# The backward half of the scan's decay weight, formed on VectorE instead of GpSimd

## The chip, the cores and the metric

The kernel runs on one core of a Trainium2 chip. The metric is the device time of one execution in microseconds (us), taken as the median of several runs. A core has five engines that run side by side, each through its own instruction list in order: TensorE (PE in the profile; PEld is its weight load), VectorE (DVE), ScalarE (ACT), GpSimd (POOL) and SyncE (SP), which here only issues DMA transfers. An engine that waits holds up everything behind the waiting instruction in its own list.

## The reference

One inference step of a four-layer backbone over 384 tokens (128 context tokens and 256 latent ones, model width 1024). Layers 0 and 3 mix tokens with a two-way state-space scan (SSD), layer 1 with a short convolution, layer 2 with differential attention; a gated convolutional FFN follows each. For the scan the reference forms, for each chunk of 128 tokens and each of 32 heads, a forward pass

```
decay  = exp(where(mask, acs[q] - acs[s], -inf))      # acs: running sum of dt * a
cb     = einsum('bcqgn,bcsgn->bcqsg', c, b)           # per group of four heads
y_diag = einsum('bcqsgr,bcsgrp->bcqgrp', cb[..., None] * decay * dt[:, :, None], x)
y_off  = einsum('bcqgn,bcgrpn->bcqgrp', c, h_in) * exp(acs)[..., None]
```

and the same again backward over the flipped sequence with its own `dt`, and adds the two. The kernel merges both directions: for one chunk and four heads it needs a weight `w = (cb_lower * dt_fwd + cb_upper * dt_bwd) * e`, 128 by 512, with `e` the exponential of the decay.

## The kernel before

All matrix weights are streamed from memory in blocks of 128x1024 floats. Each is split into a high and a low part (`wh` on ACT at L155, `wl` on DVE at L156), and every product of the projections is three matmuls (L340, 24 of them for an output block of 128x384). Four rotating buffers hold raw blocks.

An SSD layer runs eight groups of four heads. While `scan` works on group g, the projections of group g+1 (four blocks that go through the three-tap convolution, L396 on ACT, L398 and L400 on DVE) and the gate of group g (two blocks) run on PE between the scan's small products. The blocks of all of these rotate through three PSUM banks (`mm`), and a bank is free for the next 24 matmuls when the convolution's last DVE instruction (L400) has read it.

`decay(t)`, called for the three chunks of a group, forms the weight: the backward product of the masked `cb` and the backward `dt` (L683), four exponents (L686 on DVE, L687 on ACT), four multiply-adds of the forward half (L690), and the product with `e` (L691). For t = 1 and 2 it also scales the carried-in states' factors (`ab`, L695 on ACT and L697 on DVE). `out` multiplies the weights with the tokens (L726, `yp`). `e` and `w` share one tag of four buffers.

Besides this, the adaLN modulation of the next layers is computed as filler: `unit` (L187, `modps`, four 512-column matmuls, eight records in the trace) reads a 1 MB block of `w_mod`. In the SSD stage all of these blocks pass through one buffer (`wm`, `WM = 1`), so a block can be loaded only when PE has read the one before it. The filler is dealt out evenly by `pace`, a call per group, but the order on every engine is not the order of the code: the program is built with `TileContext(nc, schedule_with_timeline_sim=True)` (L1017), and a scheduler in the build orders all engines' instructions by its own estimate of times. It therefore moves instructions of other engines too when one instruction changes its engine.

DMA transfers are issued by SP in that scheduled order: weight blocks, `wm`, the rows of `acs` (`ab`), carried-in states (`h`), and the writing of new states (`out_new_state`).

Of the kernel before, what the change touches and what calls it, by code (L numbers as in the profile page):

```python
# [14 lines left out]
ALU = mybir.AluOpType  # L15
# [4 lines left out]
P = 128  # L20
# [24 lines left out]
class Net:  # L45
# [570 lines left out]
    def ssd_core(self, l, j, keep, cw, dn, y, ssq):  # L616
        d, V, S, GP, PE = self.d, self.V, self.S, self.GP, self.PE
        h4 = lambda a: a.rearrange("p (h e) -> p h e", h=4)

        def convs(g, pr, out, tag="mm"):  # L620

            ch = self.cm_weights(2)
            for b in range(2):
                ps = self.cm_block(ch, 2, b, tag=tag)
                w = cw[:, g, 2 * pr + b]
                t = self.conv(ps, w)
                S.activation(t, t, AF.Silu, bias=w[:, 3:4])
                out.append(t)
                yield
# [20 lines left out]
        def scan(g, blocks):  # L650
# [22 lines left out]
            cb = pl.tile([P, 2, NT, P], F32, tag="cb", name="cb")  # L673
# [5 lines left out]
            def decay(t):  # L679

                per = lambda a, dr: a[:, t, dr * 32 + 4 * g:dr * 32 + 4 * g + 4, None].to_broadcast([P, 4, P])
                e, w = tt("e"), tt("w")
                GP.tensor_tensor(h4(w), cb[:, 1, t, None, :].to_broadcast([P, 4, P]), per(dt, 1), op=ALU.mult)  # L683
                for h in range(4):
                    hs, sl = 4 * g + h, slice(h * P, (h + 1) * P)
                    V.scalar_tensor_tensor(e[:, sl], abs_[t][:, 0, sl], dac[:, t, hs:hs + 1], abs_[t][:, 1, sl], op0=ALU.subtract, op1=ALU.min)  # L686
                    S.activation(e[:, sl], e[:, sl], AF.Exp, bias=nac[:, t, hs:hs + 1])  # L687
                for h in range(4):
                    hs, sl = 4 * g + h, slice(h * P, (h + 1) * P)
                    V.scalar_tensor_tensor(w[:, sl], cb[:, 0, t, :], dt[:, t, hs:hs + 1], w[:, sl], op0=ALU.mult, op1=ALU.add)  # L690
                V.tensor_tensor(w, w, e, op=ALU.mult)  # L691
                mv = [(xt[:, t, :], w)]
                if t:
                    ce = abs_[t]
                    S.activation(ce, ce, AF.Exp)  # L695
                    c3 = ce.rearrange("p r (h q) -> p (r h) q", h=4)
                    V.tensor_tensor(c3, c3, Cc[:, None, t * P:(t + 1) * P].to_broadcast([P, 8, P]), op=ALU.mult)  # L697
                    mv += [(hst[t, dr], ce[:, dr]) for dr in range(2)]
                return mv
# [31 lines left out]
            states(((1, 0), (2, 1)))  # L731
            hst.update({(1, 0): hin[0], (2, 0): new[0], (2, 1): hin[1], (1, 1): new[1]})
            mv0 = decay(0)
            yield
            states(((0, 0), (0, 1)))
            mv1 = decay(1)
            yp = [self.psum("yp") for _ in range(2)]
            out(0, mv0)
            mv2 = decay(2)
            yield  # L740
            out(1, mv1)
# [7 lines left out]
        with self.tc.tile_pool(name=f"steps{l}", bufs=1, reuse_waits="tile") as sp:  # L749
            dt, dac, nac, gd, wdt, dec = self.steps(j, keep, sp, lambda: list(convs(0, 0, cur)) + list(convs(0, 1, cur, "yp")))  # L750
# [273 lines left out]
```

## Time and profile before

| | us |
|---|---|
| median of three runs | 2422.38 (2415.94 to 2424.57) |
| the profiled execution | 2417.66 |
| its span in the profile | 2415.9 |
| PE busy | 2295.4 (95%) |
| DVE busy | 1621.2 (67%) |
| ACT busy | 1253.4 (52%) |
| POOL busy | 334.2 (14%) |

The profile is one execution, 1.8 us longer than its span. The two SSD stages lie at about 46 to 392 us and 1745 to 2083 us; the rest of the span is FFN, short convolution, attention and output projections, in which the changed line does not occur. A row of a timeline gives start, duration, engine, line, operation and, in brackets, how long the engine stood idle before it and what released it. Consecutive matmuls overlap, so a PE row's duration is longer than its distance to the next one.

### The profile page before, as it was taken

To read this page: it belongs to the slowest core of one execution; us is meant where nothing else is said; L and a number is where in the kernel's file an instruction comes from. 1 tells how busy PE (TensorE), PEld (TensorE's weight loads), DVE (VectorE), ACT (ScalarE), POOL (GpSimd) and SP (SyncE) were. 2 spreads that over 40 slices of the span, in tenths; PEclk is the share of its full clock that TensorE was granted. 3 is DMA by queue.
4 is the path that set the end of the run, shared out by engine and by line. 5 is a ranking of instruction groups with operands and counts; after the bars stand their busy time and mean duration, and the time that the engine had idled before them with its cause. 6 is when DMAs were issued, how large, how long until landed. Compare 5 with 4: busy or idle time off the path is not lost.

```text
span 2415.9 us, 35621 instructions
## 1 busy us (share of the span) xinstructions
PE 2295.4 (95%) x13132; PEld 2002.2 (83%) x13132; DVE 1621.2 (67%) x2930; ACT 1253.4 (52%) x2173; POOL 334.2 (14%) x498
## 2 busy tenths in 40 slices
PE   6989999899999999999999979999998999989998
PEld 3878887699987969998688649998687888779987
DVE  3787876577655457776655547776578888677765
ACT  3666765444444344444544444444556776554444
POOL 1122330100001010000123320000113323010000
PEclk7999999999999999999999999999999999989999
DMA  7556655533537564335435463335455654423442
GB/s 286 181 162 207 202 192 177 201 132 122 166 111 288 204 245 138 125 122 166 155 106 176 155 244 107 123 127 162 147 159 171 200 159 153 139 97 123 131 146 81
DMA packets 113374, 391.79 MB, mean 162 GB/s; under 512 B 13104, under 2 KB 25520, under 8 KB 100912
## 3 DMA queue, kind: packets, MB, share of 16 engines
q1 hardware_dynamic: 113200, 389.52, 49.2%
q8 instruction: 103, 1.69, 0.3%
q14 instruction: 71, 0.58, 0.1%
HBM read 382.39 MB, written 7.08 MB: 161 GB/s over the span
## 4 chain that ended last, share of the span: by engine, by line
PE 78%; DVE 9%; DMA 6%; ACT 3%; issue 2%; POOL 2%; SPq 0%; POOLq 0%; ACTq 0%; DVEq 0%
PE mm L340 44%; PE mm L380 20%; PE mm L811 4%; DMA wm<-in_w_mod 3%; PE modps L187 2%; PE yp L380 2%; DVE e L686 2%; DVE wl L156 1%; PE yp L726 1%; DVE w L690 1%; PE yp L852 1%; ACT jk L263 1%; DVE cv L398 1%; DMA wx<-in_w_mod 1%; PE yp L340 1%
## 5 line engine op out<-in xcount | busy, mean ns | idle before, releaser
L340 PE MATMUL mm<-hh,wh 128*128 128x384 f32 (+1 forms) x2352 | 796.4, 340 | 14.9 <-DVE cv L400 9.8
L340 PE MATMUL mm<-hl,wh 128*128 128x384 f32 (+1 forms) x2352 | 793.8, 338 | 0.0
L340 PE MATMUL mm<-hh,wl 128*128 128x384 f32 (+1 forms) x2352 | 792.0, 338 | 0.0
L156 DVE TENSOR_TENSOR wl<-wr,wh 128x1024 fp32r<-128x1024 f32 (+2 forms) x466 | 564.4, 1213 | 259.7 <-ACT wh L155 257.6
L155 ACT ACTIVATE wh<-wr 128x1024 fp32r<-128x1024 f32 (+2 forms) x466 | 483.3, 1039 | 313.1 <-PE mm L340 243.9
L340 PEld LDWEIGHTS mm<-hh,wh 128*128 128x128 f32 (+1 forms) x2352 | 443.3, 189 | 38.9 <-DVE cv L400 14.6
L340 PEld LDWEIGHTS mm<-hh,wl 128*128 128x128 f32 (+1 forms) x2352 | 442.3, 188 | 5.3 <-issue 3.4
L340 PEld LDWEIGHTS mm<-hl,wh 128*128 128x128 f32 (+1 forms) x2352 | 442.6, 188 | 4.5 <-issue 2.2
L396 ACT ACTIVATE cv<-mm,fcw 128x384 f32<-128x384 f32 x176 | 100.1, 571 | 233.4 <-PE mm L340 228.2
L380 PE MATMUL mm<-wh,gh 128*128 128x512 f32 x528 | 208.7, 395 | 0.0
L380 PE MATMUL mm<-wl,gh 128*128 128x512 f32 x528 | 208.6, 395 | 0.0
L380 PE MATMUL mm<-wh,gl 128*128 128x512 f32 x528 | 207.9, 395 | 0.0
L271 POOL TENSOR_SCALAR m<-s 128x1 f32<-128x1 f32 x42 | 17.2, 409 | 1145.5 <-ACT jk L263 1144.7
L398 DVE SCALAR_TENSOR_TENSOR cv<-mm,fcw,cv 128x127 f32<-128x127 f32 x352 | 144.1, 410 | 42.6 <-ACT cv L396 42.6
L405 ACT ACTIVATE gh<-fg 128x384 fp32r<-128x384 f32 x176 | 92.2, 524 | 152.6 <-PE mm L380 151.7
L406 DVE TENSOR_TENSOR gl<-fg,gh 128x384 fp32r<-128x384 f32 x176 | 97.6, 557 | 96.7 <-ACT gh L405 96.1
L400 DVE SCALAR_TENSOR_TENSOR cv<-mm,fcw,cv 128x127 f32<-128x127 f32 x352 | 145.8, 415 | 10.8
L380 PEld LDWEIGHTS mm<-wh,gh 128*128 128x128 f32 x528 | 99.0, 187 | 25.0 <-issue 0.8
L380 PEld LDWEIGHTS mm<-wh,gl 128*128 128x128 f32 x528 | 99.0, 187 | 24.2
L380 PEld LDWEIGHTS mm<-wl,gh 128*128 128x128 f32 x528 | 99.0, 187 | 23.9
L187 PE MATMUL modps<-wm,sil 128*32 128x512 f32 x496 | 78.3, 655 | 18.5 <-DMA wm<-in_w_mod 17.6
L683 POOL TENSOR_TENSOR w<-cb,dt 128x512 f32<-128x512 f32 x48 | 71.6, 1504 | 92.5 <-DVE w L691 91.6
(224 smaller groups left out, 3180.9 us busy)
## 6 DMA issues: line engine op xcount, KB each, us to landing
wr<-in_ffn_up SPq DMA_DIRECT2D x176, 512.0 KB
wm<-in_w_mod SPq DMA_DIRECT2D x62, 1024.0 KB
wr<-in_ssd_in SPq DMA_DIRECT2D x96, 512.0 KB
wr<-in_ffn_down SPq DMA_DIRECT2D x88, 512.0 KB
wx<-in_w_mod SPq DMA_DIRECT2D x34, 1024.0 KB
ab<-acs SPq DMA_DIRECT2D x48, 512.0 KB
wr<-in_ssd_out SPq DMA_DIRECT2D x32, 512.0 KB
wr<-in_sc_in SPq DMA_DIRECT2D x32, 384.0 KB
```

The costliest lines, as they stand in the source:

```text
L155: self.S.activation(hi[:, :m], raw[:, :m], AF.Copy)
L156: self.V.tensor_tensor(lo[:, :m], raw[:, :m], hi[:, :m].bitcast(F32), op=ALU.subtract)
L187: self.PE.matmul(acc[32 * j:32 * j + 32, :], self.sil[:, kb, :], raws[:, j // 2, (j % 2) * 512:(j % 2 + 1) * 512], start=kb == 0, stop=kb ...
L340: self.PE.matmul(acc[:m], w, h, start=n == 0, stop=n == len(ops) - 1)
L380: self.PE.matmul(acc[t], g[:, o:o + n], w, start=k == 0 and i == 0, stop=k == nk - 1 and i == 2)
L396: self.S.activation(t, src, AF.Copy, scale=cw[:, 1:2])
L398: self.V.scalar_tensor_tensor(t[:, o + 1:o + n], src[:, o:o + n - 1], cw[:, 0:1], t[:, o + 1:o + n], op0=ALU.mult, op1=ALU.add)
L400: self.V.scalar_tensor_tensor(t[:, o:o + n - 1], src[:, o + 1:o + n], cw[:, 2:3], t[:, o:o + n - 1], op0=ALU.mult, op1=ALU.add)
L405: self.S.activation(hi, src, AF.Copy)
L406: self.V.tensor_sub(lo, src, hi.bitcast(F32))
L683: GP.tensor_tensor(h4(w), cb[:, 1, t, None, :].to_broadcast([P, 4, P]), per(dt, 1), op=ALU.mult)
L811: PE.matmul(acc[t][:, :256], h[k][:, o:o + m], w[:, ws], start=k == 0 and i == 0, stop=k == KB - 1 and i == 2)
```

## The change

In `decay` the first product moves from GpSimd to VectorE; operands, result and buffer are the same. It occurs 48 times: three chunks, eight groups, two layers. GpSimd keeps the state products (L707, L717) and the sum of squares (L648).

```
-                GP.tensor_tensor(h4(w), cb[:, 1, t, None, :].to_broadcast([P, 4, P]), per(dt, 1), op=ALU.mult)
+                V.tensor_tensor(h4(w), cb[:, 1, t, None, :].to_broadcast([P, 4, P]), per(dt, 1), op=ALU.mult)
```

The scheduler then orders all engines anew. Three places show how.

The first is VectorE in layer 3, fifth group, the part of its list that ends with the release (the last L400 here) of the bank that PE's next 24 matmuls need. Before:

```order
L398 SCALAR_TENSOR_TENSOR cv<-mm,cw,cv 128x127
L690 SCALAR_TENSOR_TENSOR w<-cb,dt,w 128x128 x4
L400 SCALAR_TENSOR_TENSOR cv<-mm,cw,cv 128x127
L398 SCALAR_TENSOR_TENSOR cv<-mm,cw,cv 128x255
L686 SCALAR_TENSOR_TENSOR e<-ab,dac 128x128 x4
L156 TENSOR_TENSOR wl<-wr,wh 128x1024
L400 SCALAR_TENSOR_TENSOR cv<-mm,cw,cv 128x127
L398 SCALAR_TENSOR_TENSOR cv<-mm,cw,cv 128x255
L400 SCALAR_TENSOR_TENSOR cv<-mm,cw,cv 128x255
```

Now:

```order
L398 SCALAR_TENSOR_TENSOR cv<-mm,cw,cv 128x127
L400 SCALAR_TENSOR_TENSOR cv<-mm,cw,cv 128x127
L398 SCALAR_TENSOR_TENSOR cv<-mm,cw,cv 128x255
L683 TENSOR_TENSOR w<-cb,dt 128x512
L156 TENSOR_TENSOR wl<-wr,wh 128x1024
L686 SCALAR_TENSOR_TENSOR e<-ab,dac 128x128 x4
L400 SCALAR_TENSOR_TENSOR cv<-mm,cw,cv 128x127
L398 SCALAR_TENSOR_TENSOR cv<-mm,cw,cv 128x255
L400 SCALAR_TENSOR_TENSOR cv<-mm,cw,cv 128x255
L156 TENSOR_TENSOR wl<-wr,wh 128x1024
L398 SCALAR_TENSOR_TENSOR cv<-mm,cw,cv 128x127
L690 SCALAR_TENSOR_TENSOR w<-cb,dt,w 128x128 x4
```

The third chunk's product (L683) stands in this piece now, and the third chunk's four multiply-adds (L690) have gone behind the release. The products of the first two chunks stand earlier in the same group, each ahead of its exponents (L686).

The second place is TensorE in layer 3, second group; `wm_17795` and `wm_18171` are two successive blocks of the one `wm` buffer, `mm_17299` is the next projection block. Before:

```order
L187 MATMUL modps_17040<-wm_17795,sil_83 32x512 x4
L726 MATMUL yp_17219<-w_17202,xt_17059 64x128 x2
L726 MATMUL yp_17220<-w_17202,xt_17059 64x128 x2
L726 MATMUL yp_17219<-ab_17051,h0_17055 64x128 x2
L726 MATMUL yp_17220<-ab_17051,h0_17055 64x128 x2
L726 MATMUL yp_17219<-ab_17051,s_17137 64x128 x2
L726 MATMUL yp_17220<-ab_17051,s_17137 64x128 x2
L340 MATMUL mm_17299<-hh0_16119,wh_16948 128x384
L340 MATMUL mm_17299<-hl0_16121,wh_16948 128x384
```

Now:

```order
L187 MATMUL modps_17040<-wm_17795,sil_83 32x512 x4
L726 MATMUL yp_17219<-w_17202,xt_17059 64x128 x2
L726 MATMUL yp_17220<-w_17202,xt_17059 64x128 x2
L726 MATMUL yp_17219<-ab_17051,h0_17055 64x128 x2
L726 MATMUL yp_17220<-ab_17051,h0_17055 64x128 x2
L726 MATMUL yp_17219<-ab_17051,s_17137 64x128 x2
L726 MATMUL yp_17220<-ab_17051,s_17137 64x128 x2
L187 MATMUL modps_17040<-wm_18171,sil_83 32x512 x4
L726 MATMUL yp_17219<-w_17226,xt_17059 64x128 x2
L726 MATMUL yp_17220<-w_17226,xt_17059 64x128 x2
L726 MATMUL yp_17219<-ab_17053,s_17134 64x128 x2
```

Before, the projection follows the state products at once and the unit of `wm_18171` comes in the next group; now that unit, and the third chunk's products behind it, stand ahead of the projection.

The third place is TensorE in layer 3, fourth group, between the third and the fourth projection block. Before:

```order
L726 MATMUL yp_17971<-w_17954,xt_17811 64x128 x2
L726 MATMUL yp_17972<-w_17954,xt_17811 64x128 x2
L340 MATMUL mm_18051<-hh1_16120,wl_17838 128x384
L726 MATMUL yp_17971<-ab_17803,h0_17807 64x128 x2
L726 MATMUL yp_17972<-ab_17803,h0_17807 64x128 x2
L726 MATMUL yp_17971<-ab_17803,s_17889 64x128 x2
L726 MATMUL yp_17972<-ab_17803,s_17889 64x128 x2
L668 MATMUL tp_18189<-ident_120,cv_17872 128x128 x3
L187 MATMUL modps_17040<-wm_18547,sil_83 32x512 x4
L340 MATMUL mm_18109<-hh0_16119,wh_17843 128x384
```

Now:

```order
L668 MATMUL tp_18189<-ident_120,cv_17872 128x128 x3
L187 MATMUL modps_17040<-wm_19299,sil_83 32x512 x4
L726 MATMUL yp_17971<-w_17893,xt_17811 64x128 x2
L726 MATMUL yp_17972<-w_17893,xt_17811 64x128 x2
L726 MATMUL yp_17971<-w_17954,xt_17811 64x128 x2
L726 MATMUL yp_17972<-w_17954,xt_17811 64x128 x2
L726 MATMUL yp_17971<-ab_17803,h0_17807 64x128 x2
L726 MATMUL yp_17972<-ab_17803,h0_17807 64x128 x2
L726 MATMUL yp_17971<-ab_17803,s_17889 64x128 x2
L726 MATMUL yp_17972<-ab_17803,s_17889 64x128 x2
L187 MATMUL modps_17040<-wm_19523,sil_83 32x512 x4
L340 MATMUL mm_18109<-hh0_16119,wh_17843 128x384
```

Before there is one unit in this group; now there are two, with eight rows of `yp` products between them. The same shape (two units with only these products between) arises once in layer 0, in its fourth group. In five more groups a second unit now stands 24 projection matmuls behind the first. In layer 0's second group the third chunk's products now stand ahead of the projection block `mm_1263`, which they followed before.

## Rows read from the trace of the kernel before

**Rows 1.** Four regular groups: stretch, us, busy PE, PEld, DVE, ACT, POOL, clock, DMA.

```profile
1864.00:2005.10 141.10, 137.90 (x925) 124.46 (x924) 117.81 (x240) 99.12 (x166) 44.54 (x45) 1.00 0.59 179
```

**Rows 2.** Chain that ended last, layer 3's fourth group: start us, us, what.

```profile
1897.54 1.02 DVE cb L675 x2
...
1916.29 4.43 PE mm L340 x24
```

**Rows 3.** Waits of PE in layer 3's SSD stage: us in total, times, longest us.

```profile
PE mm L340 <- DVE cv L400: 4.0, 5, 0.8
```

**Rows 4.** Waits of PE in layer 0's SSD stage.

```profile
PE mm L340 <- DVE cv L400: 4.5, 4, 1.4
```

**Rows 5.** Groups by line and shape: busy us, mean ns, idle before them.

```profile
L686 DVE SCALAR_TENSOR_TENSOR e<-ab,dac 128x128 f32<-128x128 f32 x192 | 81.5, 483 | 0.0
L683 POOL TENSOR_TENSOR w<-cb,dt 128x512 f32<-128x512 f32 x48 | 71.6, 1504 | 92.5 <-DVE w L691 91.6 <-DVE cb L675 0.9
...
L691 DVE TENSOR_TENSOR w<-w,e 128x512 f32<-128x512 f32 x48 | 38.8, 814 | 9.2 <-ACT e L687 9.2
```

**Rows 6.** Timeline of VectorE, layer 3's fourth group.

```profile
1899.12 1.75 DVE L686 SCALAR_TENSOR_TENSOR e<-ab,dac 128x128 f32<-128x128 f32 x2
...
1901.46 1.65 DVE L686 SCALAR_TENSOR_TENSOR e<-ab,dac 128x128 f32<-128x128 f32 x6
...
1906.66 0.68 DVE L691 TENSOR_TENSOR w<-w,e 128x512 f32<-128x512 f32 x1
1907.26 1.21 DVE L156 TENSOR_TENSOR wl<-wr,wh 128x1024 fp32r<-128x1024 f32 x1
...
1908.66 1.26 DVE L691 TENSOR_TENSOR w<-w,e 128x512 f32<-128x512 f32 x1
...
1911.24 1.13 DVE L690 SCALAR_TENSOR_TENSOR w<-cb,dt,w 128x128 f32<-128x128 f32 x4
```

**Rows 7.** Timeline of GpSimd, the same group.

```profile
1898.64 2.09 POOL L683 TENSOR_TENSOR w<-cb,dt 128x512 f32<-128x512 f32 x2
```

**Rows 8.** Chain that ended last, layer 3's second group: a reload of `wm` and what follows.

```profile
1827.90 8.28 DMA wm<-in_w_mod
...
1836.22 1.94 PE modps L187 x8
1838.16 2.76 PE yp L726 x24
```

**Rows 9.** Timeline of PE, layer 0: two units 6.3 us of PE work apart.

```profile
282.18 1.06 PE L187 MATMUL modps<-wm,sil 128*32 128x512 f32 x8
...
290.94 1.06 PE L187 MATMUL modps<-wm,sil 128*32 128x512 f32 x8 [0.84 <-DMA wm<-in_w_mod]
```

**Rows 10.** Chain that ended last, whole span: other reloads, and layer 0's second group.

```profile
73.72 7.05 DMA wm<-in_w_mod
...
141.77 4.44 PE mm L340 x24
146.21 1.46 PE yp L726 x24
...
217.83 9.44 DMA wm<-in_w_mod
```

**Rows 11.** Busy time by stretch around the reload of rows 8.

```profile
1829.00:1834.00 5.00, 0.20 (x2) 0.20 (x4) 5.00 (x17) 2.07 (x5) 0.18 (x1) 0.74 0.73 245
...
1838.00:1841.00 3.00, 3.00 (x29) 2.58 (x25) 2.96 (x11) 2.73 (x5) 0.00 (x0) 0.50 0.27 83
```

**Rows 12.** Timeline of PE, layer 3's fourth group, from the state products on.

```profile
1911.97 0.66 PE L726 MATMUL yp<-w,xt 128*64 128x128 f32 x8
...
1914.43 1.06 PE L187 MATMUL modps<-wm,sil 128*32 128x512 f32 x8
1916.29 0.44 PE L340 MATMUL mm<-hh,wh 128*128 128x384 f32 x1 [0.80 <-DVE cv L400]
```

**Rows 13.** Timeline of VectorE, layer 0's second group, the third chunk's weight.

```profile
142.39 0.69 DVE L691 TENSOR_TENSOR w<-w,e 128x512 f32<-128x512 f32 x1 [1.90 <-ACT e L687]
```

## The prediction

> **What bounds the kernel now.** I read the busy time by stretch first, then the chain of waits, then who PE waits for, and last the timelines of the two engines that the product moves between. In four regular groups of layer 3's scan, 141.1 us, PE is busy for 137.9 us and VectorE for 117.8 us [rows 1]: PE is nearly full and VectorE is at 83%. The chain still runs through both. In each group it leaves PE with the `cb` masks (1897.54) and comes back at 1916.29, when the next 24 projection matmuls start [rows 2]. Over those 18.7 us VectorE works without a pause, and PE, busy with other blocks, arrives early by only 0.80 us [rows 12]. So the reader is to see two engines that finish almost together. All that PE waits for the convolution's bank (L400) is 4.0 us in layer 3's stage and 4.5 us in layer 0's [rows 3, 4]. A faster VectorE can give back 8.5 us and no more; anything that holds PE is paid almost whole.
>
> **The product itself.** 48 products leave GpSimd, 71.6 us of its busy time [rows 5], and join VectorE. VectorE has no row with such operands. The nearest is L691, same size and type, two SBUF inputs: 0.68 us long and 0.60 us from its start to the next start (1906.66 to 1907.26) [rows 6]. From above I bound it by 1.05 us, half of the two GpSimd products that ran in 2.09 us [rows 7]. From below there is no reason for less than L691 costs. I take L691's 0.60, three in a group: +1.8 us.
>
> **What VectorE gets back.** While GpSimd ran its two products (1898.64 to 1900.73), two L686 took 1.75 us; the next six took 1.65 us, 0.275 each [rows 6, 7]. Without GpSimd's products the two should take 0.55 us, so 1.2 us come back. The second L691 took 1.26 us against 0.68 for the first: 0.6 us more. That is 1.8 us in a group, as much as the product costs. The total says the same: L686 at 0.275 would need 52.8 us and not 81.5, L691 at 0.68 would need 32.6 and not 38.8; 34.9 us come back against 28.8 (48 at 0.60) to 50.4 (48 at 1.05). VectorE's load stays about equal.
>
> The Trainium skill ("SBUF — State Buffer", section "Who interferes with whom") says that a VectorE instruction with two SBUF inputs contends with a GpSimd instruction that reads SBUF, and that the one that comes second is blocked for the other's whole length. The trace agrees on the contention (0.87 us against 0.275 for an L686). By whole blocking the 48 products would give back up to 48 times 1.05, about 50 us of VectorE, an estimate; the rows show 34.9, and PE's 8.5 us caps both.
>
> The order changes too. In the stretch that ends with the bank's release, the third product comes in and the third chunk's four multiply-adds go behind the release; they took 1.13 us, 1.05 from start to start. The stretch becomes 18.7 + 1.8 - 1.8 - 1.05 = 17.7 us. That is below PE's own arrival, so most of the 8.5 us of waiting goes. I count -6 us for it, and -2 us because the state products now stand in fewer pieces between projections; bounds 0 and -10.5.
>
> **What the new order costs.** The filler units read one buffer. A unit cannot start until the block before it has been read and the next one has landed. Reloads in the chain took 7.05, 8.28 and 9.44 us [rows 8, 10]. The tightest regular pair had its second unit start 7.7 us after the end of the first (283.24 to 290.94), after a wait of 0.84 us with 6.3 us of PE work in between [rows 9]. I take 7.7 us, bounds 7.05 and 9.44. Five effects follow, all on PE, whose list is in order:
>
> - Layer 3, second group. The unit of `wm_17795` ended at 1838.16 and the state products at 1840.92 [rows 8]; projections followed at once. Now the next unit stands there. It cannot start before 1838.16 + 7.7 = 1845.9: PE idles 4.9 us (4.3 to 6.7). The clock is still low: it was 0.74 over the idle stretch 1829 to 1834 and 0.50, the 1.2 GHz level, over 1838 to 1841 [rows 11], and an idle PE will keep it there. At that level a unit took 1.94 us [rows 8] and not the 1.06 of rows 9, and 24 state products took 2.76 us and not the 1.46 of rows 10. So the unit and the 24 state products behind the new wait cost about 0.9 + 1.3 = 2.2 us more. Sum 7.1 us.
> - Layer 3, fourth group, the pair of `wm_19299` and `wm_19523`. Between them stand 24 state products, some 2.0 us by the distance 1911.97 to 1914.43 less a transpose [rows 12]. PE idles 7.7 - 2.0 = 5.7 us, of which 0.8 was idle before: 4.9 us. Five idle microseconds brought the clock down in rows 11, so 2.2 us more: 7.1 us. The second unit's own time is no addition, since another group loses it.
> - Layer 0, fourth group, the same shape: 7.1 us.
> - Five pairs with 24 projection matmuls and the state products between them, about 6.4 us of work. At the 0.84 us of rows 9 each this is 4.2 us, of which 0.84 existed already. Net 3.4 us (-0.8 to 14).
> - Layer 0, second group. The projection that ran from 141.77 [rows 10] now follows the third chunk's products, whose weight was ready at 142.39 + 0.69 = 143.08 [rows 13]: 1.3 us.
>
> **Sum.** 7.1 + 7.1 + 7.1 + 3.4 + 1.3 = 26.0 us, less 8 us, is +18.0 us. On the profiled execution (2417.66 us; its span is 2415.9) this gives 2435.7 us. The median of the three runs lies 4.7 us above that execution, so from there it would be 2440.4. I forecast 2437 us, between the two. With the lower bounds (7.05 us, no clock loss, nothing at the five pairs and in layer 0's second group) the three large waits are 4.3 + 4.25 + 4.25 = 12.8 us, less 10.5: 2420. With the upper (9.44 us: 8.9 + 8.8 + 8.8 + 14 + 1.3, nothing back) it is +42: 2460.
>
> **Rivals.**
>
> Faster: the reloads are hidden. If SP issues each block the moment its buffer is free, with fewer transfers beside it, and PE reaches the second unit later than I think because it is held by VectorE there, the waits fall where PE was idle anyway. Then the 8.5 us come back, and the two starts of the scan, where VectorE's exponents ran slow beside GpSimd too, may give 3 us each: 2403 us. For it: 34.9 us of VectorE time really is freed. Against it: PE arrives at the bank's release only 0.80 us early, so no idle time of 5 us is there to hide a reload in. It decides if a reload takes under 3 us; no row shows one.
>
> No change: gains and waits cancel. With reloads at 7.05 us and the clock kept, the sum above is +2.3 us, about 2420 to 2425.
>
> VectorE becomes the bound. If the broadcast operand makes the product 1.05 us on VectorE and the remaining GpSimd work keeps L686 slow, a group gains 3.15 us, less 1.05 for the moved multiply-adds and 0.8 for the idle now there: +1.3 us in some twelve groups, 16 us on top of the waits: 2453 us. The 83% of rows 1 speaks for it, the relief of 1.8 us in rows 6 against it.
>
> The Trainium skill ("Perfetto Trace Analysis", section "Optimizing Scalar/DVE Operations") says that work of a saturated VectorE may be offloaded, even to GpSimd, but that between those two it might not help because they share a read port. The change does the reverse, and the first half speaks against it: by it alone, 48 products at 0.60 us, 28.8 us, would fall on VectorE with nothing back, an estimate that leads to the rival just told. The rows side with the second half.
>
> **Chances.** What a measurement can tell from no change is 0.5%, 12 us, so 2410.3 to 2434.5. The forecast, waits above 12 us net, 0.50; no change, 0.30; VectorE as the bound, 0.11; faster, 0.09. The first reaches down to 2428, so I give 0.04 of it to "same": slower 0.57, same 0.34, faster 0.09. Range 2419 to 2455: it takes in the no-change case and the price of a bound VectorE, and leaves out the faster case.
>
> **What would show it.** In the profile after: no L683 on GpSimd; L683 on VectorE at 0.6 to 0.7 us; L686's mean near 0.30 and not 0.483; VectorE's busy time within 15 us of before; PE's waits for L400 well under 8.5 us; PE's waits for `wm` in the scan stages above 15 us, three of them of 4 us or more, with the clock at 0.50 behind them. The prediction is wrong if the waits for `wm` stay under 8 us in sum, if PE waits longer for VectorE than before, or if L683 takes over 0.9 us there.

## The result, and the profile after

Measured side by side, the changed kernel takes 2435.17 us (median of 5, 2427.65 to 2436.41) and the kernel before 2419.89 us (5, 2415.94 to 2424.57): ratio 1.0059, 95% interval 1.0044 to 1.0074. The forecast was 2437 us. The profiled execution of the changed kernel took 2435.8 us, its span is 2434.0, 18.1 us more than before.

The first view is the groups by line on VectorE, after (busy us, mean ns, idle before). It answers [rows 5].

```profile
L686 DVE SCALAR_TENSOR_TENSOR e<-ab,dac 128x128 f32<-128x128 f32 x192 | 59.7, 364 | 0.0
L683 DVE TENSOR_TENSOR w<-cb,dt 128x512 f32<-128x512 f32 x48 | 34.7, 722 | 0.2
L691 DVE TENSOR_TENSOR w<-w,e 128x512 f32<-128x512 f32 x48 | 32.6, 680 | 2.2 <-ACT e L687 2.2
```

The product has come (34.7 us). L686 gave back 21.8 us and L691 6.2. VectorE's whole busy time is 1621.8 us against 1621.2. The load is the same, as forecast. That L686 gets its time back because GpSimd no longer multiplies beside it is shown by the runs with fixed order below: it takes 60.1 us in all with the product on VectorE in the old order (e1), and 85.9 with the product on GpSimd in the new order (e2). L691's gain came with the order as well, for e2 has it too:

```profile
L686 DVE SCALAR_TENSOR_TENSOR e<-ab,dac 128x128 f32<-128x128 f32 x192 | 85.9, 503 | 0.0
...
L691 DVE TENSOR_TENSOR w<-w,e 128x512 f32<-128x512 f32 x48 | 32.5, 678 | 3.7 <-ACT e L687 3.7
```

Next, the six group intervals of layer 3's scan from the second group's `cb` masks to the eighth's, before and then after, in the columns of [rows 1] (stretch, its length, busy PE, PEld, DVE, ACT, POOL, granted clock, DMA).

```profile
1818.88:2037.87 218.99, 208.51 (x1372) 184.43 (x1370) 182.27 (x367) 150.23 (x255) 69.56 (x71) 0.98 0.59 177
```

```profile
1822.77:2055.68 232.91, 209.79 (x1390) 191.29 (x1390) 183.64 (x384) 143.04 (x247) 47.32 (x52) 0.93 0.53 165
```

13.9 of the 18.1 us lie here. VectorE is busy 1.4 us longer, PE 1.3 us, so the rest is idle PE. What it waits for in layer 3's stage, after (us in total, times, longest), and the two lines of before that [rows 3] does not have:

```profile
PE modps L187 <- DMA wm<-in_w_mod: 10.3, 4, 3.8
PE mm L340 <- DVE cv L400: 8.8, 4, 3.2
PE modps L187 <- DMA wx<-in_w_mod: 4.8, 1, 4.8
PE yp L726 <- DVE w L691: 4.0, 3, 3.2
```

```profile
PE yp L726 <- DVE w L691: 5.2, 1, 5.2
...
PE modps L187 <- DMA wm<-in_w_mod: 3.3, 2, 2.0
```

The reader is to see two growths: 7.0 us of waits for `wm`, which were forecast, and 4.8 us of waits for L400, which were forecast to shrink. The third new line, 4.8 us for a block of another modulation buffer (`wx`), lies at 1745 us, ahead of the first group; e9 below has no such wait and loses as much in this stage. The timeline of PE, after, shows the places (layer 3's second, fourth, fifth and seventh group; answers to [rows 8, 12]):

```profile
1833.86 0.99 PE L726 MATMUL yp<-w,xt 128*64 128x128 f32 x8 [3.21 <-DVE w L691]
1838.60 1.94 PE L187 MATMUL modps<-wm,sil 128*32 128x512 f32 x8 [3.75 <-DMA wm<-in_w_mod]
...
1846.02 1.94 PE L187 MATMUL modps<-wm,sil 128*32 128x512 f32 x8 [2.72 <-DMA wm<-in_w_mod]
...
1926.36 1.94 PE L187 MATMUL modps<-wm,sil 128*32 128x512 f32 x8 [3.07 <-DMA wm<-in_w_mod]
...
1964.89 0.69 PE L340 MATMUL mm<-hh,wh 128*128 128x384 f32 x1 [3.20 <-DVE cv L400]
...
2038.48 0.44 PE L340 MATMUL mm<-hh,wh 128*128 128x384 f32 x1 [3.20 <-DVE cv L400]
```

These three units took 1.94 us and not 1.06. Over the second group's two the granted clock is 0.50, its lower level, 1.2 GHz (answers [rows 11]):

```profile
1834.00:1841.00 7.00, 3.25 (x22) 1.18 (x22) 7.00 (x17) 5.35 (x13) 2.11 (x1) 0.50 0.35 137
1841.00:1848.00 7.00, 4.28 (x32) 2.21 (x30) 5.52 (x13) 2.67 (x4) 0.61 (x1) 0.50 0.81 274
```

The filler units of layer 3 are bunched now: three in the second group where two stood, two in the third and fourth where one stood, and none in the fifth to seventh where one stood. The length of each group, from the start of its first `cb` matmul (L672) to the next group's, shows what that made of the time (us, one execution each; e1, e9, e10 and e12 are runs described below):

| group of layer 3 | 2nd | 3rd | 4th | 5th | 6th | 7th |
|---|---|---|---|---|---|---|
| before | 42.5 | 35.3 | 35.3 | 35.3 | 35.3 | 35.3 |
| after | 46.2 | 37.4 | 37.7 | 37.7 | 35.9 | 38.0 |
| e1 | 38.7 | 35.5 | 35.5 | 35.5 | 35.5 | 35.5 |
| e9 | 45.0 | 36.6 | 37.7 | 37.7 | 35.9 | 38.0 |
| e10 | 41.6 | 35.5 | 35.5 | 35.5 | 35.5 | 35.5 |
| e12 | 46.5 | 35.5 | 40.8 | 37.1 | 44.5 | 37.1 |

Of the 13.9 us, 8.3 are in the three groups that got a unit more; the three units' own work is some 3 of these. The other 5.6 are in the three groups that lost their unit and became longer all the same.

### The profile page after: what moved, and what is told of

Same layout as the page of the kernel before. It is cut to its first block, busy times and chain, and to the rows that moved or that the text cites. A ratio compares the mean times of both kernels' runs of the same rounds, so it can differ in the third digit from the quotient of the medians.

```text
span 2434.0 us, 35563 instructions
## 1 busy us (share of the span) xinstructions
PE 2301.7 (95%) x13132; PEld 2014.4 (83%) x13132; DVE 1621.8 (67%) x2978; ACT 1238.2 (51%) x2159; POOL 268.8 (11%) x450
## 4 chain that ended last, share of the span: by engine, by line
PE 82%; DVE 6%; DMA 5%; ACT 3%; POOL 2%; issue 2%; SPq 0%; POOLq 0%; ACTq 0%; DVEq 0%
PE mm L340 47%; PE mm L380 20%; PE mm L811 4%; PE modps L187 3%; PE yp L380 2%; DMA wm<-in_w_mod 2%; PE yp L726 1%; PE yp L852 1%; DMA h<-in_state 1%; ACT jk L263 1%; DVE wl L156 1%; DMA wx<-in_w_mod 1%; POOL r L273 1%; DVE e L686 1%; PE sp L708 1%
## 5 line engine op out<-in xcount | busy, mean ns | idle before, releaser
L396 ACT ACTIVATE cv<-mm,fcw 128x384 f32<-128x384 f32 x176 | 100.1, 572 | 232.9 <-PE mm L340 227.8
L400 DVE SCALAR_TENSOR_TENSOR cv<-mm,fcw,cv 128x127 f32<-128x127 f32 x352 | 146.1, 416 | 10.9
L811 PE MATMUL mm<-wh,hh 128*128 128x256 f32 x288 | 83.4, 290 | 0.0
```

Source lines behind the costliest of these rows:

```text
L396: self.S.activation(t, src, AF.Copy, scale=cw[:, 1:2])
L400: self.V.scalar_tensor_tensor(t[:, o:o + n - 1], src[:, o + 1:o + n], cw[:, 2:3], t[:, o:o + n - 1], op0=ALU.mult, op1=ALU.add)
L811: PE.matmul(acc[t][:, :256], h[k][:, o:o + m], w[:, ws], start=k == 0 and i == 0, stop=k == KB - 1 and i == 2)
```

## Experiments

Two theories are to be told apart. Order: moving the product is neutral for VectorE, and the time goes with the new order of instructions that the scheduler chose. Load: VectorE's added work makes the groups longer. To separate them, most kernels below have each engine's list fixed: the traced instructions carry the same names in both kernels, so a list of names per engine can be chained.

```
     with tile.TileContext(nc, schedule_with_timeline_sim=True) as tc:
         build(tc, d)
+        pin(tc)    # for each engine: every instruction behind the one listed before it
+    # tc.add_manual_dep(ins[name], prev, DependencyInfo(DependencyClass.NoSync, DependencyReason.DATA))
```

Such an edge only orders the issue. No run fixes the old order of the kernel before without another edit; the nearest, e8, moves two units and takes 1.0000 of the kernel before, so the fixing itself costs nothing that shows. "Old order" and "new order" are the lists of the kernel before and of the changed kernel. Ratios are to the kernel before, run on the same chip.

| run | product on | order | median us (n) | ratio, 95% |
|---|---|---|---|---|
| changed kernel | VectorE | new | 2435.2 (5) | 1.0059, 1.0044 to 1.0074 |
| e1 | VectorE | old | 2420.4 (11) | 1.0008, 1.0000 to 1.0017 |
| e2 | GpSimd | new | 2438.7 (6) | 1.0085, 1.0070 to 1.0100 |
| e3 | VectorE | new, quarter blocks | 2421.4 (11) | 1.0015, 1.0006 to 1.0024 |
| e4 | GpSimd | old, quarter blocks | 2408.2 (5) | 0.9963, 0.9949 to 0.9976 |
| e5 | VectorE | new, ScalarE edited | 2436.2 (6) | 1.0074, 1.0058 to 1.0089 |
| e6 | VectorE | new, units apart | 2428.4 (8) | 1.0046, 1.0030 to 1.0061 |
| e7 | VectorE | new, e5 and e6 | 2430.1 (12) | 1.0045, 1.0032 to 1.0058 |
| e8 | GpSimd | old, units apart | 2418.0 (12) | 1.0000, 0.9990 to 1.0010 |
| e9 | VectorE | new in layer 3's scan only | 2432.8 (6) | 1.0056, 1.0042 to 1.0069 |
| e10 | VectorE | new in layer 0's scan only | 2419.6 (11) | 1.0003, 0.9994 to 1.0012 |
| e11 | VectorE | old; ScalarE and GpSimd new in layer 3 | 2447.8 (4) | 1.0120, 1.0107 to 1.0134 |
| e12 | VectorE | old, units of layer 3 bunched | 2442.0 (4) | 1.0104, 1.0089 to 1.0118 |

**e1 and e2: engine against order.** Edits: the changed kernel with the old lists, each product standing on VectorE where the old program lists it; the kernel before with the new lists.

> The product on VectorE, but every engine's list in the order that the kernel before has (each product stands where that program lists it). Before is 2420 us, the changed kernel 2435. If the loss comes from the new order (my theory), this run is 2414 to 2424 us, like before: the product's cost and the end of the contention cancel. If VectorE's added work is what lengthens the groups (rival), it is 2430 to 2440, like the changed kernel, with PE's waits for L400 and L691 in the scan stages grown by 8 us or more.

> The product back on GpSimd, but every engine's list in the order that the changed kernel has. By the order theory it keeps the loss: 2430 to 2442 us, with the waits for wm in the scan stages near the changed kernel's 18.4 us (8.1 in layer 0, 10.3 in layer 3). By the rival (VectorE's load) the loss goes with the product: 2415 to 2424.

The order theory holds on both sides. With the old order the move of the product costs 0.08%, 2 us. With the product back on GpSimd the new order costs 0.85%; the lists were made for a product on VectorE, so some of this may be mismatch, and the new order's own price is rather the 0.51% between the changed kernel and e1, 12 us. In e1's regular groups PE's wait for the bank is 1.02 us (0.80 before, [rows 12]), and the groups are 0.22 us longer:

```profile
1954.70 0.44 PE L340 MATMUL mm<-hh,wh 128*128 128x384 f32 x1 [1.02 <-DVE cv L400]
```

**e3 and e4: the reload made short.** Every `wm` block is loaded as a quarter.

```
-            self.load(raw, d["w_mod"][l, s, kb])
+            self.load(raw[:, 0, :512], d["w_mod"][l, s, kb, :, 0, :512])   # for wm
-                               raws[:, j // 2, (j % 2) * 512:(j % 2 + 1) * 512],
+                               raws[:, 0, :512],                              # for wm
```

> The changed kernel in its own order, but each wm block is loaded as a quarter (128x512) and the unit's four matmuls all read that quarter, so the modulation is computed from other weights; the reload is short. If the reloads behind the units are the loss (my theory), the 18.4 us of waits for wm in the scan stages fall below 4 us, the clock behind them stays up, and the time falls by 17 to 24 us, to 2411 to 2418; it then stands within 5 us of the kernel before with the same short blocks. If only half of the loss hangs on the reloads and the rest on other changes of the order (groups 5 to 7 of layer 3, attention), it is 2418 to 2426 and 8 us or more above. If VectorE's load is the loss, 2428 to 2435.

> The kernel before in its own order with the same quarter blocks (modulation computed from other weights). It had 8.2 us of waits for wm in the scan stages (4.9 and 3.3), so by the reload theory it falls by 6 to 10 us, to 2410 to 2414. The difference to the changed kernel with short blocks is what hangs on neither the reload's length nor its place.

Both fall by about as much (0.44 and 0.37%), so 0.52% still stands between the two orders, 13 us. This is the second case of e3's expectation, and the reload's length is not the loss by itself. Waits of PE in layer 3's stage in e3 (its lines L695 and L404 are L691 and L400 of the other kernels), and its second group:

```profile
PE mm L344 <- DVE cv L404: 9.1, 5, 3.2
PE yp L730 <- DVE w L695: 8.3, 4, 4.0
...
PE modps L190 <- DMA wm<-in_w_mod: 2.1, 2, 1.3
```

```profile
1829.72 1.12 PE L730 MATMUL yp<-w,xt 128*64 128x128 f32 x8 [3.42 <-DVE w L695]
1835.53 1.07 PE L190 MATMUL modps<-wm,sil 128*32 128x512 f32 x8 [1.31 <-DMA wm<-in_w_mod]
1840.63 1.12 PE L730 MATMUL yp<-w,xt 128*64 128x128 f32 x8 [4.03 <-DVE w L695]
```

The waits for `wm` went from 10.3 to 2.1 us and those for L691 rose from 4.0 to 8.3. In the second group the weights are late in any case; the units only waited in their shadow.

**e9 and e10: which stage.** Between the two scans both programs have long stretches in the same order, so the order can be changed in one stage alone.

> The product on VectorE as in e1 (2420 us, old order); only the instructions of layer 3's scan stage stand in the new order, everything else in the old one. By the marks in the traces (+14 of the +18 us fall in that stage) it is 2431 to 2436 us. If the stage only shows what was set up earlier, or the loss is spread over the program, it is under 2427.

> As e9, but with layer 0's scan stage in the new order and the rest in the old one. By the marks (+4 to +5.5 us) 2423 to 2426 us; together with e9 it should add up to the 15 us between e1 and the changed kernel. If the stages interact, the two losses do not add up within 4 us.

All of it is layer 3: 1.0056 against e1's 1.0008 is 0.48%, 11.6 us. Layer 0's new order costs nothing that can be measured (1.0003 against 1.0008), where 3 to 6 us more than e1 were expected. The two with the engine's 0.08% add up to 0.51% of the 0.59 measured. Yet layer 0 has waits of its own in the changed kernel, one of them the longest in the scan; PE, layer 0's fourth group, after:

```profile
220.85 1.94 PE L187 MATMUL modps<-wm,sil 128*32 128x512 f32 x8 [6.55 <-DMA wm<-in_w_mod]
```

The group around this wait is no longer for it: from L672 to L672 it takes 45.7 us after, 46.6 before, and 43.2 in e10, where the wait is 4.53 us.

**e12: bunching alone.** In the old order three units of layer 3 are moved up on PE, nothing else.

```
-PE: L187 x4 (unit) | 188 to 227 others | L187 x4 (unit)       one unit in a group
+PE: L187 x4 (unit) | 12, 40, 24 others | L187 x4 (unit)       two units, then a group without
```

> As e1 (old order, one filler unit in a group of layer 3), but on PE three units of layer 3 are moved up behind the one before (12, 40 and 24 instructions behind it), so that three groups have two and three have none, as in the changed kernel. If bunching is the loss (the second unit waits for its block, and the groups left without a unit wait for VectorE instead), 2426 to 2431 us, with 5 us or more of waits for wm and up to 1 us more of waiting for L400 in each emptied group. If the loss is in VectorE's list, 2419 to 2423.

It costs 0.96% over e1, 23 us, more than expected. The six intervals in e1 and in e12:

```profile
1825.07:2041.45 216.38, 207.17 (x1372) 183.51 (x1371) 181.73 (x384) 150.53 (x254) 45.06 (x52) 0.99 0.58 178
```

```profile
1819.40:2060.86 241.46, 217.06 (x1371) 190.88 (x1370) 181.56 (x384) 150.86 (x254) 45.09 (x52) 0.94 0.51 159
```

The same instructions and about the same VectorE time; PE takes 9.9 us longer over its own work, with the granted clock at 0.94 and not 0.99, and stands idle 15.2 us longer. PE's timeline in e12, the three second units and the three emptied groups:

```profile
1842.85 1.94 PE L187 MATMUL modps<-wm,sil 128*32 128x512 f32 x8 [3.73 <-DMA wm<-in_w_mod]
...
1885.70 0.45 PE L340 MATMUL mm<-hh,wh 128*128 128x384 f32 x1 [2.02 <-DVE cv L400]
...
1930.95 1.07 PE L187 MATMUL modps<-wm,sil 128*32 128x512 f32 x8 [2.31 <-DMA wm<-in_w_mod]
...
1962.06 0.44 PE L340 MATMUL mm<-hh,wh 128*128 128x384 f32 x1 [2.02 <-DVE cv L400]
```

```profile
2009.20 1.93 PE L187 MATMUL modps<-wm,sil 128*32 128x512 f32 x8 [5.62 <-DMA wm<-in_w_mod]
...
2043.61 0.45 PE L340 MATMUL mm<-hh,wh 128*128 128x384 f32 x1 [2.02 <-DVE cv L400]
```

Every group that lost its unit waits 2.02 us for the bank and not 1.02: the unit had filled one microsecond that PE must wait for VectorE anyway. The last reload took 10.15 us, in the chain of waits of e12:

```profile
1999.01 10.15 DMA wm<-in_w_mod
```

**e5 to e7: mending the new order.** e5 moves, at three places on ScalarE, two exponents and L695 ahead of a Silu; e6 moves three second units later on PE; e7 does both.

```
-ACT: L687 L687 | L627 L714 | L687 L687 L695
+ACT: L687 L687 | L687 L687 L695 | L627 L714
-PE:  unit | 12 or 16 others | unit
+PE:  unit | 40 to 48 others | unit
```

> The changed kernel in its own order except on ScalarE, at three places (one group in layer 0, two in layer 3): there two of a chunk's four exponents and the factor of L695 stood behind a convolution's Silu (L627) and so behind two table loads of 1.28 us; now they stand ahead of it. If these places are why VectorE releases the bank late (theory), PE's two waits of 3.20 us for L400 in layer 3 fall to about 0.8 and the time falls by 5 to 8 us, to 2427 to 2431. If VectorE is late from its own load (rival), the waits stay near 3 us and the time within 2 us of 2435.

> The changed kernel in its own order except on PE: the three filler units that follow the one before at 12 to 16 instructions (L0 4th group, L3 2nd and 4th) are moved behind the next projection block, 40 to 48 instructions behind it. In the changed kernel they waited 6.55, 2.72 and 3.07 us for their block. If these waits are lost time, as my prediction had it, all three go and the time falls by 10 to 15 us (with the clock that comes back behind them), to 2420 to 2426. If VectorE's weights are late there anyway (rival; with short blocks PE waited 4.0 us for L691 in L3's 2nd group instead), only layer 0's and the 4th group's go: 5 to 9 us, 2426 to 2431.

> Both edits of e5 and e6 in the changed kernel's order. If these two causes are most of the loss, the time is 2416 to 2424 us, no slower than the kernel before by 0.2%. If some other part of the new order carries the loss, it stays above 2428.

e5 regained nothing (the rival of its expectation), and its wait in the fifth group is 3.86 us. The reason is in the two timelines. After (VectorE, then ScalarE, fifth group):

```profile
1958.28 1.23 DVE L697 TENSOR_TENSOR ab<-ab,cv 128x1024 f32<-128x1024 f32 x1 [1.87 <-ACT ab L695]
```

```profile
1953.10 1.28 ACT L627 ACT_TABLE_LOAD   x1
...
1955.30 1.28 ACT L687 ACT_TABLE_LOAD   x1
```

and e5, the same:

```profile
1960.66 0.35 DVE L398 SCALAR_TENSOR_TENSOR cv<-mm,cw,cv 128x127 f32<-128x127 f32 x1 [1.90 <-ACT cv L396]
```

```profile
1959.77 0.38 ACT L714 ACTIVATE s<-sp 128x256 f32<-128x256 f32 x1 [2.33 <-DMA out_new_state<-s]
```

VectorE stands idle for 1.9 us either way. Freed of the table loads, ScalarE comes to its second state copy (L714) early, waits 2.33 us for the write of the first, and the next convolution block (L396) stands behind it. One reason was removed and the next took its place. e6's interval is 0.13% below the changed kernel's, and the two intervals overlap, so its gain is not established, and neither is that of e7 (0.14% below, overlapping too). e6's waits for `wm` in layer 3 fell from 10.3 to 4.7 us, those for L400 rose to 11.1:

```profile
PE mm L340 <- DVE cv L400: 11.1, 5, 3.2
PE yp L726 <- DVE w L691: 5.7, 4, 3.4
PE modps L187 <- DMA wm<-in_w_mod: 4.7, 2, 3.8
```

It moved the units inside the same three groups; the groups without one stayed without. By e7's expectation some other part of the new order carries the loss. The profiled executions of e6 and e7 were their shortest (2421.07 and 2421.85 us), so their traces say less than the medians.

**e8: the same in the old order.** The two closest pairs are set 40 and 44 instructions apart, as in e6's diff.

> The kernel before (product on GpSimd, its own order) except on PE: the two closest pairs of units (second groups of layer 0 and layer 3, 4 and 8 instructions apart, waits of 2.56 and 1.30 us) are moved apart to 40 and 44. If a unit's wait behind its reload is lost time, it falls by 2.5 to 5 us, to 2412 to 2417; if VectorE's weights end later than the unit there, no change.

No change. What PE waited for `wm` it then waited for L691 (6.1 us in layer 3 against 5.2).

**e11: ScalarE's list alone.** Layer 3's lists of ScalarE and GpSimd from the new order, all others old.

> As e1, but ScalarE's and GpSimd's lists in layer 3's scan stage are those of the changed kernel, while PE, VectorE and SP keep the old order. If ScalarE's list (Silu and table loads between exponents) makes VectorE late, 2426 to 2430 us with PE's waits for L400 up by 4 us or more. If it does not (as e5 suggests), 2418 to 2423.

This is the slowest of all, far above the 2426 to 2430 us expected, with the second group's weights 8.84 us late:

```profile
1840.30 1.12 PE L726 MATMUL yp<-w,xt 128*64 128x128 f32 x8 [8.84 <-DVE w L691]
```

This shows how far ScalarE's list can hold VectorE up; but ScalarE's new list was made for the other engines' new lists, so it prices a mismatch and not the new list. Its expectation is met in direction and answers less than it was meant to.

## Why the prediction was right, and where it was not

- *VectorE's load stays equal.* Right: 1621.8 against 1621.2 us, and by e1 2 us in all. The product took 722 ns in the mean where 0.60 us from start to start was taken (0.68 long for most), and L686 and L691 gave back 28.0 us where 34.9 was estimated and the whole blocking of the prediction's second estimate would have given some 50. The Trainium skill ("SBUF — State Buffer", section "Who interferes with whom") has the one of VectorE and GpSimd that comes second blocked, whichever it is. The trace agrees in that GpSimd now pays too: its L707 went from 706 to 811 ns, before and after, and is 710 in e2, in the new order with the product on GpSimd:

```profile
L707 POOL TENSOR_TENSOR xw<-xt,wdt 128x256 f32<-128x256 f32 x64 | 44.4, 706 | 144.6 <-ACT xt L669 77.2 <-DVE wl L156 49.1 <-PE sp L708 18.2
```

```profile
L707 POOL TENSOR_TENSOR xw<-xt,wdt 128x256 f32<-128x256 f32 x64 | 50.9, 811 | 145.3 <-ACT xt L669 77.4 <-DVE wl L156 47.1 <-PE sp L708 20.6
```

- *The time goes with the new order of the filler units.* Right that it goes with the order: e1, e2 and e9 show it. That it is the units' order is shown only as far as that bunching units is enough for a loss of this size (e12), with waiting for the block, slower work of PE at a lower clock, and no gain in the emptied groups. Against it as the whole cause stands e3, which keeps 13 us of loss with 2.1 us of waits for `wm` in layer 3.
- *Layer 0's terms, 7.1 and 1.3 us.* Wrong. The wait came as forecast (6.55 us), and by e10 and the group's length it costs nothing: the wait of 1.28 us for L400 at 216.49 us before, in the same group, is gone after.
- *Layer 3's second group, 7.1 us.* Too large. PE idled 9.7 us at its three waits (3.21 + 3.75 + 2.72), where before it was 6.5 (5.17 and 1.30). The group grew by 3.7 us, 1.1 of them the added unit. e3 shows that L691 would hold it anyway. What the prediction's first rival says, that waits fall where PE was idle anyway, was right at this place.
- *Layer 3's fourth group, 7.1 us.* Idle 3.07 us, since this reload took 4.86 us and not 7.7; with the slow unit (1.94 us and not 1.06) some 4 us, and the group grew by 2.4. In all six intervals PE's own work grew by 1.3 us only, where 4.4 us of lost clock were put into the two sums. From the chain of waits, after:

```profile
1921.45 4.86 DMA wm<-in_w_mod
1926.36 1.94 PE modps L187 x8
```

- *Five pairs, 3.4 us net.* The 6.3 us of work in rows 9 were misread: from 283.24 to the start of the wait at 290.10 it is 6.9. The term was too large: only two such waits show on PE's timeline after, one in each layer.

```profile
264.15 1.06 PE L187 MATMUL modps<-wm,sil 128*32 128x512 f32 x8 [0.54 <-DMA wm<-in_w_mod]
...
1893.23 1.06 PE L187 MATMUL modps<-wm,sil 128*32 128x512 f32 x8 [0.77 <-DMA wm<-in_w_mod]
```

- *"The second unit's own time is no addition, since another group loses it."* Wrong. The group that loses its unit waits for VectorE in its place: in e12 the emptied groups are 0 to 1.6 us longer than in e1, not 1 us shorter.
- *The gain of 8 us.* This step failed. The waits for L400 rose by 4.8 us in layer 3. The fifth to seventh group have no unit any more (1 us each by e12), and in the fifth and the seventh, where PE waits 3.20 us, VectorE stands idle 1.87 us for ScalarE (L695). That VectorE's stretch would shorten to 17.7 us was read from VectorE's list alone; it became longer by waiting for ScalarE. That ScalarE's list is the cause is read from the trace and not shown by a run, since e5 put another wait of the same length in its place.
- *The signs named.* Of the three signs of being wrong, one came true: PE waits longer for VectorE than before, 23.6 us for L400 and L691 in the two scan stages against 18.4. The waits for `wm` came to 18.4 us as forecast (above 15), but one of them, not three, reached 4 us.

So the sum of +18 was met by terms too large on one side (26) and a gain on the other (8) that turned into a loss. The direction and its reason, the order, were foreseen; that the time came within 2 us of the forecast is luck. What is left open is how the 11.6 us of layer 3 divide between the units and ScalarE's list. The group lengths give an idea of it, from one execution each: against e10, whose layer 3 has the old order, e9's three groups with a unit more are 6.6 us longer and its three emptied groups 5.0, where e12, with the old list of ScalarE, shows 3.2 for three emptied groups. A kernel with the new lists and one unit a group would tell; it was not run.

The Trainium skill ("ScalarE: Activation LUTs", section "Table sets: the hidden batching unit") advises to batch activations by table set. The changed kernel does: 52 loads at L687, L627 and L636 against 66 (31, 28 and 7). What the fewer loads are worth is not priced here: the kernel became slower for other reasons, ScalarE is busy for 51% of the span, and two of the remaining loads stood on the path, where taking them off it gained nothing (e5). The groups after:

```profile
L687 ACT ACT_TABLE_LOAD x24 | 30.8, 1283 | 0.4
L627 ACT ACT_TABLE_LOAD x23 | 29.5, 1283 | 10.9 <-DVE cv L400 10.6
L636 ACT ACT_TABLE_LOAD x5 | 6.4, 1283 | 0.1
```

## What to carry to other kernels

When a scheduler orders the program, price an edit as two changes, the instruction and the order, and measure them apart by fixing the lists; here the instruction was worth 2 us and the order 12 or more. Filler work is worth most where an engine has to wait anyway: here one piece in each gap cost nothing, a second piece behind the same buffer waited for its block, and a gap left without its piece was idle instead. A wait that is long in a profile is not yet a loss: ask what the engine would wait for next.

## What was not expected of the hardware

The product with two broadcast operands cost no more than the plain one on VectorE (median 680 ns, as L691's). Reloads of the same 1 MB block took from 4.86 to 10.15 us. And the longer executions of one kernel tend to show the lower granted clock: twelve of e7 lie between 2421.85 us at 0.974 and 2437.73 us at 0.966, and 25 of the kernel before on the same chip between 2411.74 and 2423.22 us, at 0.973 to 0.978. Whether the clock makes the time or the idle time the clock, these runs do not tell.
